# Adaptive max pooling over 1-D signals: the long store moves to ScalarE's queue, behind a 4-byte copy

## The chip, the cores and the metric

The kernel runs on one core of a Trainium2 chip. The metric is device time in microseconds (us), the median of several runs; three runs of the kernel before gave 334.86 to 335.0. The profile is one execution on the same kind of core, recorded by the hardware profiler.

## The reference

```python
batch, channels, length, output_size = 32, 256, 4096, 256
for i in range(output_size):
    start = int(i * length / output_size)
    end = int((i + 1) * length / output_size)
    result[:, :, i] = np.max(x[:, :, start:end], axis=-1)
```

The length is a multiple of the output size, so every output is the maximum of 16 neighbouring float32 values. The input has 134.2 MB, the output 8.4 MB.

## The kernel before

The input is looked at as 2,097,152 windows of 16 values. 128 partitions take 16,384 windows each; a "column" below is one window of every partition, so there are 16,384 columns to load, reduce and store.

The columns form two groups. Group A has 13,436 columns: a first small load of 128, twelve loads of 1024 and one of 1020. Group B has 2,948: two loads of 1024 and a last load of 900. In each group a partition's columns lie side by side in memory, so that a load, or a store, of a group is one DMA with 128 rows, one per partition, and each of the 16 DMA engines moves eight of the rows.

All loads are issued by SyncE (SP; line 87 for the first, line 96 for the others) into one SBUF tile, `ring`, which holds two full loads and two gaps of 152 columns. A load starts in one half of the ring, and every second time it is moved by the gap, so that it overlaps only a part of what the load two before it left there. VectorE (DVE) reduces each load with `pooled` (line 56) in two instructions, of 872 and 152 columns, in the order in which the load after next needs the space. A load is issued as soon as the larger of these two parts of the load two before it has been reduced. The maxima go to a second tile, `kept`; those of the last load (`last_kept`) go into free space of `ring`.

There are three stores. The long one holds group A's 13,436 columns (53,744 bytes per partition), the short one the two full loads of group B (2,048 columns), and the last one the last load's 900 columns. The first two are issued by SP at the end of the program, line 117, in the order in which `stores` lists them; the last one by ScalarE (ACT), line 114. On SP the long store stands directly behind the last load, since its own data is complete by then:

```python
    nc.scalar.dma_start(out=og[:, full : full + last], in_=last_kept)
    tc.no_sync_barrier()
    for dst, src in stores:
        nc.sync.dma_start(out=dst, in_=src)
```

`no_sync_barrier` keeps the order of the program's lines for the scheduler and adds no wait between engines. The profile calls SP's DMA queue q1 and ScalarE's q10.

Of the kernel before, what the change touches and what calls it, by code (L numbers as in the profile page):

```python
# [1 line left out]

# [4 lines left out]


@with_exitstack
def kernel(  # L10
    ctx: ExitStack,
    tc: tile.TileContext,
    x: bass.AP,
    output_size: bass.AP,
    out: bass.AP,
):

    nc = tc.nc
    P = nc.NUM_PARTITIONS
    fp32 = mybir.dt.float32

    B, C, L = x.shape
    O = int(output_size)  # L30
    assert L % O == 0, (L, O)
    W = L // O
    total = B * C * O // P
    assert B * C * O % P == 0

    CHUNK = 1024
    GAP = 152
    FIRST = 128
    LOADS_A, LOADS_B = 13, 2

    LESS = 4
    group_a = [FIRST] + [CHUNK] * (LOADS_A - 1) + [CHUNK - LESS]
    last = total - sum(group_a) - LOADS_B * CHUNK
    group_b = [CHUNK] * LOADS_B + [last]
    assert 0 < last and last * (W + 1) <= CHUNK * W

    pool = ctx.enter_context(tc.tile_pool(name="pool", bufs=1))
    ring = pool.tile([P, 2 * (CHUNK + GAP) * W], fp32, tag="ring", name="ring")
    kept = pool.tile([P, total - last], fp32, tag="kept", name="kept")

    xw = x.flatten_outer_dims().rearrange("r (o w) -> (r o) w", w=W)
    ow = out.flatten_outer_dims().rearrange("r o -> (r o)")

    def pooled(dst, at, n):

        nc.vector.reduce_max(  # L56
            out=dst,
            in_=ring[:, at * W : (at + n) * W].rearrange("p (n w) -> p n w", w=W),
            axis=mybir.AxisListType.X,
        )  # L60

    taken = 0

    def group(n):

        nonlocal taken
        span = slice(taken * P, (taken + n) * P)
        taken += n
        return (
            xw[span].rearrange("(p n) w -> p (n w)", p=P),  # L70
            ow[span].rearrange("(p n) -> p n", p=P),
        )

    stores = []
    n_loads = 0
    base = 0
    for g, loads in enumerate((group_a, group_b)):
        xg, og = group(sum(loads))
        a = sum(loads) if g == 0 else 0
        for n in loads:  # L80
            if g == 0:
                a -= n
            xn = xg[:, a * W : (a + n) * W]
            dst = kept[:, base + a : base + a + n] if n != last else None
            if n == FIRST:

                nc.sync.dma_start(  # L87
                    out=ring[:, CHUNK * W : (CHUNK + n) * W], in_=xn
                )
                pooled(dst, CHUNK, n)  # L90
            else:

                low = n_loads % 2 * (CHUNK + GAP)
                moved = n_loads // 2 % 2
                at = low + moved * GAP
                nc.sync.dma_start(out=ring[:, at * W : (at + n) * W], in_=xn)
                if n != last:
                    cut = CHUNK - GAP if moved else GAP
                    parts = [(0, cut), (cut, n)]
                    for u, v in parts if moved else parts[::-1]:  # L100
                        pooled(dst[:, u:v], at + u, v - u)
                else:
                    end = (at + CHUNK) * W
                    last_kept = ring[:, end - n : end]
                    pooled(last_kept, at, n)
                n_loads += 1
            if g:
                a += n
        full = a - last if g else sum(loads)
        stores.append((og[:, 0:full], kept[:, base : base + full]))  # L110
        base += full
    assert taken == total

    nc.scalar.dma_start(out=og[:, full : full + last], in_=last_kept)
    tc.no_sync_barrier()
    for dst, src in stores:
        nc.sync.dma_start(out=dst, in_=src)


# [1 line left out]
_INS = ['x', 'output_size']  # L121
_OUTS = [((32, 256, 256), 'float32')]

_NUMBERS = {'output_size': 256}


# [26 lines left out]
```

## Time and profile before

| | before |
|---|---|
| time, median of 3 runs | 334.9 us |
| span of the profiled execution, first to last instruction | 333.1 us |
| VectorE busy | 276.5 us (83%), 32 reductions |
| bytes over the DMA engines | 142.61 MB, mean 428 GB/s |
| the DMA engines' time in packets of q1 and q10 | 98.8% and 0.3% |
| one full load, from issue to landing | 24.0 us |
| the long store, from issue to landing | 37.2 us |
| the short store, from issue to landing | 18.1 us |
| the last store, from issue to landing | 4.2 us |

The span is all that the profile gives for its execution; the median of the runs lies 1.8 us above it. A time "from issue to landing" contains the time that a transfer stands in its queue behind others: the long store is issued 0.4 us after the last load and waits for it.

### The profile page before, as it was taken

What the parts mean: (1) busy time and instruction counts of PE and PEld (TensorE: products, weight loads), DVE (VectorE), ACT (ScalarE), POOL (GpSimd) and SP (SyncE); (2) the same over time, 40 slices, a digit from 0 to 9 for tenths busy, and PEclk for the clock granted to TensorE, in tenths of its full rate; (3) what the DMA queues carried; (4) which work ended last, traced back from release to release, by engine and by line L of the source; (5) the groups of instructions that cost most, each with busy time, mean ns of one, the idle gap of its engine ahead of it and who ended that gap; (6) DMA issues with size and microseconds to landing.
All of it is one profiled execution on the core that took longest, in us unless ns stands there. A gap on an engine that the chain in (4) does not pass through costs nothing.

```text
span 333.1 us, 113 instructions
## 1 busy us (share of the span) xinstructions
DVE 276.5 (83%) x32; POOL 0.2 (0%) x4
## 2 busy tenths in 40 slices
DVE  2009979797997979799797979979797998979993
POOL 0000000000000000000000000000000000000000
DMA  9898989899898989899898989899898989899996
GB/s 378 378 504 378 504 378 496 386 441 441 378 504 378 504 378 496 386 457 425 378 504 378 504 378 504 378 441 441 385 494 377 504 378 504 378 458 443 421 413 285
DMA packets 2880, 142.61 MB, mean 428 GB/s; under 512 B 320, under 2 KB 320, under 8 KB 448
## 3 DMA queue, kind: packets, MB, share of 16 engines
q1 hardware_dynamic: 2736, 142.15, 98.8%
q10 hardware_dynamic: 144, 0.46, 0.3%
HBM read 134.22 MB, written 8.39 MB: 428 GB/s over the span
## 4 chain that ended last, share of the span: by engine, by line
DMA 57%; DVE 36%; DVEq 5%; issue 0%; SPq 0%
DMA ring<-in_x_dram 57%; DVE kept L56 36%; DVEq L148 5%; SPq L87 0%
## 5 line engine op out<-in xcount | busy, mean ns | idle before, releaser
L56 DVE TENSOR_REDUCE kept<-ring 128x152 f32<-128x2432 f32 (+3 forms) x31 | 261.4, 8472 | 51.5 <-DMA ring<-in_x_dram 51.5
L56 DVE TENSOR_REDUCE ring<-ring 128x900 f32<-128x14400 f32 x1 | 15.1, 15144 | 0.0
L134 POOL MEMSET const-bfloat16-1.0<- 128x1 bf16 x1 | 0.1, 102 | 0.0
L134 POOL MEMSET const-uint8-127<- 128x1 uint8 x1 | 0.1, 102 | 0.0
L134 POOL MEMSET const-float32-0.0<- 128x1 f32 x1 | 0.1, 99 | 0.2 <-issue 0.2
L134 POOL MEMSET const-float32-1.0<- 128x1 f32 x1 | 0.1, 99 | 0.0
## 6 DMA issues: line engine op xcount, KB each, us to landing
ring<-in_x_dram SPq DMA_DIRECT2D x1, 8160.0 KB, 23.9
ring<-in_x_dram SPq DMA_DIRECT2D x1, 7200.0 KB, 21.6
out_dram<-kept SPq DMA_DIRECT2D x1, 6718.0 KB, 37.2
ring<-in_x_dram SPq DMA_DIRECT2D x1, 1024.0 KB, 4.7
out_dram<-kept SPq DMA_DIRECT2D x1, 1024.0 KB, 18.1
out_dram<-ring ACTq DMA_DIRECT2D x1, 450.0 KB, 4.2
ring<-in_x_dram SPq DMA_DIRECT2D x14, 24.0
```

Source lines behind the costliest of these rows:

```text
L56: nc.vector.reduce_max(out=dst, in_=ring[:, at * W : (at + n) * W].rearrange("p (n w) -> p n w", w=W), axis=mybir.AxisListType.X,)
L134: nc = _bacc.Bacc("TRN2", target_bir_lowering=False, num_devices=1)
L148: with _tile.TileContext(nc) as tc:
```

## The change

The long store moves from SP to ScalarE, and the last store from ScalarE to SP, behind the short one. The last full load (the one before the last load) is reduced in parts of 828 and 196 columns instead of 872 and 152. ScalarE first issues a DMA of 4 bytes, from the first column of that load's maxima to a new tile `gate`; it depends on the part of 828 columns, so ScalarE waits for that reduction. Behind it, ScalarE issues the long store. The long store has no dependency on the copy; only the order on ScalarE puts it behind.

```diff
+    gate = pool.tile([1, 1], fp32, tag="gate", name="gate")
...
+    OPEN = 828
...
                     cut = CHUNK - GAP if moved else GAP
+                    before_last = n_loads == LOADS_A + LOADS_B - 1
+                    if before_last:
+                        assert moved
+                        cut = OPEN
                     parts = [(0, cut), (cut, n)]
                     for u, v in parts if moved else parts[::-1]:
                         pooled(dst[:, u:v], at + u, v - u)
+                        if before_last and u == 0:
+                            nc.scalar.dma_start(out=gate[:, :], in_=dst[0:1, 0:1])
+                            tc.no_sync_barrier()
+                            nc.scalar.dma_start(out=stores[0][0], in_=stores[0][1])
...
-    nc.scalar.dma_start(out=og[:, full : full + last], in_=last_kept)
-    tc.no_sync_barrier()
-    for dst, src in stores:
-        nc.sync.dma_start(out=dst, in_=src)
+    nc.sync.dma_start(out=stores[1][0], in_=stores[1][1])
+    nc.sync.dma_start(out=og[:, full : full + last], in_=last_kept)
```

On VectorE the order of the instructions stays the same.

## The prediction

> **What bounds the kernel now.** I read the page first (shares of queues and engines), then windows over the whole span, then the timeline of the last 45 us, then the DMA queues in a short window near the end, and last the trace's DMA packet records (one for each row of a transfer on one DMA engine, with queue, start and duration) where a window is too coarse.
>
> The page, first the whole span and the engines, then the queues (packets, MB, share of 16 engines' span):
>
> ```profile
> span 333.1 us, 113 instructions
> DVE 276.5 (83%) x32; POOL 0.2 (0%) x4
> ...
> q1 hardware_dynamic: 2736, 142.15, 98.8%
> q10 hardware_dynamic: 144, 0.46, 0.3%
> ```
>
> q1 is SP's queue (all loads and two stores), q10 ScalarE's (the last store). Together they fill 99.1% of the 16 DMA engines' time over the whole span; VectorE has 17% to spare. The windows (us, DVE busy, POOL busy, clock, DMA share, GB/s) show where the other 1% is:
>
> ```profile
> 0.00:1.70 1.70, 0.00 (x0) 0.20 (x4) 1.00 0.00 0
> 1.70:2.70 1.00, 0.00 (x0) 0.00 (x0) 1.00 0.98 254
> 2.70:312.00 309.30, 260.50 (x31) 0.00 (x0) 1.00 1.00 434
> ...
> 331.70:333.06 1.36, 0.00 (x0) 0.00 (x0) 1.00 0.00 0
> ```
>
> It lies before the first packet and behind the last. In between, packet records show each engine's next row starting within 0.01 us of the end of the one before. So the span is a start of 1.7 us, a fixed amount of transfer at 434 GB/s until 331.71, 0.49 us until the last completion arrives (332.20) and 0.86 us of closing steps. Only three things can move the end: less transfer, an idle hole on the DMA engines, or a longer tail. The timeline shows what has to arrive in time for there to be no hole:
>
> ```profile
> 290.99 0.33 SPq L96 DMA_DIRECT2D ring<-in_x_dram  x1
> 291.37 21.91 SPq L117 DMA_DIRECT2D out_dram<-kept  x2
> 295.63 17.28 DVE L56 TENSOR_REDUCE kept<-ring 128x872 f32<-128x13952 f32 x2 [2.07 <-DMA ring<-in_x_dram]
> 312.82 15.14 DVE L56 TENSOR_REDUCE ring<-ring 128x900 f32<-128x14400 f32 x1
> 328.00 0.37 ACTq L114 DMA_DIRECT2D out_dram<-ring  x1
> ```
>
> The last load is issued at 290.99 and the long store 0.4 us behind it, on the same queue. By the packet records the load's eighth and last row on each engine starts at 309.50 to 310.02 and ends at 311.85 to 312.29; the load lands at 312.64. The long store then runs to 327.73 to 328.15, the short store (issued 312.94) to 330.21 to 330.60, and the last store to 331.71. It is issued at 328.00, after the last reduction, and its packets start on each engine where q1's end. This window of the queues lies wholly behind its issue:
>
> ```profile
> DMA packets 86, 0.70 MB, mean 414 GB/s; under 512 B 0, under 2 KB 0, under 8 KB 0
> ## 3 DMA queue, kind: packets, MB, share of 16 engines
> q1 hardware_dynamic: 86, 0.70, 98.8%
> ```
>
> No q10 packet runs in 328.5 to 330.2, though the first packet of the run came 1.00 us after its issue (0.73 to 1.73). The last store therefore stood ready behind q1's rows for about a second microsecond. That is the slack of the compute side: the last reduction could end some 0 to 1.2 us later without opening a hole.
>
> **The change part by part.** *Transfer.* The loads and the three stores keep their rows; each is one DMA, as before. Only the 4 B copy is new. Bytes saved: none, so nothing here gives a gain.
>
> *The 4 B copy.* It is one packet on one engine. The nearest rows are the 4 B completion writes, 0.009 us each (321 of them); the far bound is 0.91 us, the slowest packet of the run (an 8 KB row at the cold start). I take 0.01, by the size. No engine waits for the copy's data; the long store is issued behind it without waiting for its landing. The Trainium skill (DMA: Bandwidth & Descriptors, Specifications) says that a transfer under 512 B is done as a read-modify-write, which speaks against such a copy; no row here shows one, and it gives no figure.
>
> *The reductions.* The last full load is cut at 828 instead of 872 columns. From 14.686 us for 872 and 2.677 us for 152, a column costs 16.68 ns: 13.95 and 3.41 us, whose sum is unchanged at 17.36. The short store's wait and the last reduction's start (312.82) stay. Cost 0. The first part now ends at 295.63 + 13.95 = 309.58.
>
> *ScalarE's queue.* ScalarE waits for that end; behind the wait stands only the long store. A wait of this kind was followed by the issue 0.03 us later (327.97 to 328.00), an issue takes 0.37, and two issues follow each other 0.05 apart (1.10 to 1.15): copy at 309.61, long store at 310.03. Its first packets can run 1.00 us later, at 311.03 (start-up row); as an upper bound 2.21 later (328.00 to 330.21, a wait that the rows ahead explain), at 312.24. They are needed when the load's last row ends, from 311.85. The load's last row is therefore in progress on every engine when the store arrives, and the hole is 0 by the near bound and 0.39 us on the earliest engine by the far one (0.60 if that row, which ran up to 0.47 us over its usual 2.13, were not slowed). In the start-up the 16 engines' first rows were spread over 0.55 us, which puts the last arrival at 311.6, still early. I take 0.05. The cover is the load's last row; if it is gone, every microsecond of lateness is one of time. The Trainium skill (same page, Latency and other measured facts) gives a first byte of about 0.6 us for such a queue: behind the end of the issue (310.40) this is 311.0, no hole, and the sum would be 0.05 less. The start-up row agrees: 0.63 us from 1.10 to 1.73.
>
> *The slow last rows.* Ten of the 16 last load rows ran over, by 0.16 us in the mean over all 16. If the store's presence in the same queue causes it, up to 0.16 comes back; if not, 0. I take 0.
>
> *SP's queue.* It loses the long store's issue (0.43 us at 291.37, then a wait for VectorE until 312.9, so nothing came of it) and gets the last store behind the short one. The last store's issue still follows the last reduction at 328.0. Its queue mates: the short store's rows, on q1 from about 314, and the long store's on q10. In whatever order the engines serve them, they hold the same rows and run out at 330.21 to 330.60, when the last store has been ready for 0 to 1.2 us. Cost 0. What comes late next, if a hole opens, is exactly this last store.
>
> *The tail.* One more completion to be looked at: the closing waits that are already fulfilled cost 0.03 to 0.04 us each (332.26 to 332.29). I take 0.04.
>
> Sum: 0.01 + 0.05 + 0.04 = 0.10 on 333.06, so a span of 333.16. The median of the runs, 334.90, lies 1.84 above the span (there is no other time for the profiled execution), which gives 335.0. With the bounds of the hole and of the slow rows the forecast's own range is 334.7 to 335.6.
>
> **The rivals.** *A store row comes ahead of the load (slower).* With two queues an engine may take a 1.99 us row of the long store ahead of the load's last row, or ahead of the load's completion write. One engine is enough: the load lands at 314.63, the last reduction runs 314.81 to 329.95, the last store is issued at 329.98 and can run at 330.98 (or 332.19) at the earliest. The engines run out at 330.4 in the mean, so a hole of 0.6 to 1.8 us opens: 335.5 to 336.7. It decides from a landing over 0 to 1.2 us later than 312.64. For it: the store arrives some 0.6 us before the last rows end. Against it: at the end of before, rows and completion of the queue in hand all went ahead of q10. The Trainium skill (same page, Queues, rings and completion order) says that an engine changes queues only at a packet's end, typically 9 to 17 descriptors; eight rows and a completion would be one packet, which the tail agrees with. By that rule nothing gets between, and the time is the forecast's. Chance 0.14.
>
> *The copy or the hand-over is dear (slower).* The copy takes its far bound of 0.91 us on its engine, or the store comes over 0.7 us late. That engine finishes last: 335.8 to 336.0. Chance 0.07.
>
> *Two queues overlap on one engine (faster).* The store reads SBUF while the load writes it, so the store's first row could run beside the load's last: up to one row, 1.99 us, 332.9; half of it gives 333.9. For it: it would be the first time that a load and a store stand in two queues. Against it: where both queues were filled, rows of the one followed rows of the other without overlap, and the 434 GB/s is the same for loads (434) and the long store (433 in 311.84 to 327.73). The Trainium skill (same page, Issuing engines are not separate DMA queues) says that several queues interleave on the same 16 engines and gain no bandwidth; by that this chance would be 0. I give 0.07.
>
> *The holding back does not work.* If the store were issued when its own data is ready, before the last load, up to 15.9 us (its eight rows) would fall ahead of that load: about 350. Against it: in the program the copy carries the wait and stands before the store on ScalarE. Chance 0.02.
>
> **How the numbers follow.** The forecast has 0.70. I count 0.2% (0.67 us) as what a measurement of this kernel can tell from no change. Faster is the overlap, 0.07; slower is 0.14 + 0.07 + 0.02 = 0.23; the same is 0.70. The range is the forecast's, up through most of the first two rivals to 336.3, and down to 334.4, the slow rows' return with a little overlap; the deep overlap, the top of the first rival and the failed hold, under 2 in 10, are left out.
>
> **What would show it.** Right: DMA share still 1.00 to about 331.7, the long store's first rows starting within 0.01 us of the load's last, the last load landing at about 312.6, the last reduction ending at 328.0, the last store running last. The first rival: a landing at 314 or later, and a window near 330.5 with a low DMA share. The dear hand-over: a hole at 311.9 to 312.5. Overlap: over 434 GB/s around 312 and an end before 331. Wrong altogether: if the end moves over 0.7 us with the DMA engines as full as before and the same landing.

## The result and the profile after

The changed kernel takes 335.63 us, median of 17 runs, against 334.96 for 17 runs of the kernel before beside them: 1.0017 times as long, with a 95% interval of 1.0011 to 1.0024 (the medians themselves stand at 1.0020). It is slower, by 0.67 us between the medians and 0.4 to 0.8 us by the interval. The forecast was 335.0 in a range of 334.4 to 336.3. The profiled span grew by 0.84 us, from 333.06 to 333.90.

The page of the changed kernel, whole span and queues. The long store's bytes have moved from q1 to q10; VectorE works as long as before:

```profile
span 333.9 us, 114 instructions
DVE 276.5 (83%) x32; POOL 0.2 (0%) x4
...
q1 hardware_dynamic: 2736, 135.73, 94.2%
q10 hardware_dynamic: 146, 6.88, 4.8%
```

The timeline around the end of the last load (start, duration, engine, line, operation):

```profile
295.87 17.28 DVE L57 TENSOR_REDUCE kept<-ring 128x828 f32<-128x13248 f32 x2 [2.07 <-DMA ring<-in_x_dram]
309.86 1.13 ACTq L113 DMA_DIRECT2D gate<-kept  x1
311.03 1.08 ACTq L115 DMA_DIRECT2D out_dram<-kept  x1
313.06 15.14 DVE L57 TENSOR_REDUCE ring<-ring 128x900 f32<-128x14400 f32 x1
...
328.23 0.34 SPq L129 DMA_DIRECT2D out_dram<-ring  x1
```

The copy is issued when forecast (309.86 for 309.61, in an execution in which the last load was issued 0.24 us later too), but its issue lasts 1.13 us and the long store's 1.08, where 0.37 had been taken for the first. The windows (us, DVE busy, POOL busy, clock, DMA share, GB/s) show what this does. A packet counts in full where it starts, so that a short window can show a share far above 1:

```profile
2.70:311.80 309.10, 260.06 (x31) 0.00 (x0) 1.00 1.00 433
311.90:312.60 0.70, 0.70 (x1) 0.00 (x0) 1.00 0.01 0
312.60:332.42 19.82, 15.61 (x2) 0.00 (x0) 1.00 0.99 423
332.42:333.90 1.48, 0.00 (x0) 0.00 (x0) 1.00 0.00 0
```

Between 311.90 and 312.60 no row starts. By the packet records the load's last rows end at 311.89 to 312.42 (mean 312.07), and the first long rows start at 312.62 to 312.76 (mean 312.67): all 16 engines stand still, 0.60 us in the mean. The kernel before has 998 GB/s booked in the same 0.70 us:

```profile
311.90:312.60 0.70, 0.70 (x1) 0.00 (x0) 1.00 2.32 998
```

After that the engines are full to the end. They alternate between the queues row by row: from 318.6 on each engine does one long row (1.99 us), then one row of the short store (0.31 us). The queues (packets, MB, share of 16 engines) in the stretch from 316 to 330 of the changed kernel, both at work:

```profile
q10 hardware_dynamic: 96, 5.16, 85.4%
q1 hardware_dynamic: 80, 0.66, 11.0%
```

The 0.84 us of the spans can be followed through the mean ends of the rows. The load's last rows end 0.02 us later, the hole adds 0.60, and the long rows take 15.99 instead of 15.89 us in all. The short store's rows take 0.02 less and the last store's 0.03 more, which makes 0.73; the last packets end 0.75 later in the mean. The latest of them ends only 0.70 later (332.41 instead of 331.71), since the engines end closer together than before. The last landing is 0.69 later (332.89 instead of 332.20), and from there to the end it is 1.01 us instead of 0.86: 0.69 + 0.15 = 0.84.

### The profile page after: what moved, and what is told of

It is laid out like the page before. It is cut to its first block, busy times and chain, and to the rows that moved or that the text cites. A ratio compares the mean times of both kernels' runs of the same rounds, so it can differ in the third digit from the quotient of the medians.

```text
span 333.9 us, 114 instructions
## 1 busy us (share of the span) xinstructions
DVE 276.5 (83%) x32; POOL 0.2 (0%) x4
## 4 chain that ended last, share of the span: by engine, by line
DMA 57%; DVE 36%; DVEq 5%; issue 0%; SPq 0%
DMA ring<-in_x_dram 57%; DVE kept L57 36%; DVEq L160 5%; SPq L93 0%
## 5 line engine op out<-in xcount | busy, mean ns | idle before, releaser
L57 DVE TENSOR_REDUCE kept<-ring 128x152 f32<-128x2432 f32 (+5 forms) x31 | 261.4, 8473 | 51.7 <-DMA ring<-in_x_dram 51.7
```

The source lines that it names most:

```text
L57: nc.vector.reduce_max(out=dst, in_=ring[:, at * W : (at + n) * W].rearrange("p (n w) -> p n w", w=W), axis=mybir.AxisListType.X,)
```

## The experiments

All times are medians beside runs of the kernel before on the same chip. The open question was what opens the hole: that the store comes late, that ScalarE issues it, the copy, or the second queue. ScalarE and its queue q10 go together in every run here, so those two can't be told apart.

**An earlier store.**

```diff
-    OPEN = 828
+    OPEN = 764
```

> The last full load is cut at 764 columns instead of 828, so that the 4 B copy and the long store are issued 64 x 16.68 ns = 1.07 us earlier. Late hand-over (my theory: in the changed kernel the DMA engines stood still from 311.9 to 312.6 because the long store's first rows came too late): first long rows ready by 311.6, no hole, the span 0.6 us shorter and the time 335.0 to 335.1, within 0.2 of the kernel before. Rival, a store row ahead of the load: the earlier store gets rows in front of the load's last ones, the last load lands about 2 us later and the time is 335.6 or more. Rival, two queues cost something by themselves: the hole goes but the time stays at 335.6.

Measured: 335.95 against 335.09, ratio 1.0026 (1.0016 to 1.0035). The hole is gone and the time has not come back. The issues are earlier as planned, and the long rows start at 311.75 to 312.43, directly behind the load's; but these first 16 rows last 2.84 us in the mean instead of 1.99. The timeline, then windows; no row starts in 312.60 to 314.40, since all the first ones are still under way:

```profile
308.88 1.13 ACTq L113 DMA_DIRECT2D gate<-kept  x1
310.05 0.48 ACTq L115 DMA_DIRECT2D out_dram<-kept  x1
```

```profile
311.90:312.60 0.70, 0.70 (x1) 0.00 (x0) 1.00 3.52 1075
312.60:314.40 1.80, 1.80 (x2) 0.00 (x0) 1.00 0.00 0
```

They end at 314.54 to 315.19; in the changed kernel, with the store issued 1 us later, they ended at 314.64 to 314.79. So the expectation's third branch held, the hole gone and the time still high. Lateness, as I had put it, isn't the whole cause: 0.86 us of slow first rows took the place of 0.60 us of hole. The load landed on time (312.94), so no row had got ahead of it.

**The copy on ScalarE itself.**

```diff
-                            nc.scalar.dma_start(out=gate[:, :], in_=dst[0:1, 0:1])
+                            nc.scalar.copy(out=gate[:, :], in_=dst[0:1, 0:1])
```

> The hold is made by a one-element copy that ScalarE computes itself, in place of the 4 B DMA; the cut stays at 828. Late hand-over: the DMA copy's issue, 1.13 us on ScalarE, is gone, and the store's issue begins about 310.1 instead of 311.0. If the store's own issue stays at 1.08 us, its first rows run at about 311.7 and the hole is 0 to 0.1; if the 1.08 was caused by the copy in front and falls to 0.4, they are ready at 311.0. Either way 335.0 to 335.2. Rival, two queues cost something by themselves: 335.6 as with the DMA copy.

Measured: 336.03 against 335.09, 1.0028 (1.0017 to 1.0038). The timeline, then windows:

```profile
309.94 0.37 ACTq L115 DMA_DIRECT2D out_dram<-kept  x1
```

```profile
311.90:312.60 0.70, 0.70 (x1) 0.00 (x0) 0.00 (x0) 1.00 3.66 1152
312.60:314.40 1.80, 1.80 (x2) 0.00 (x0) 0.00 (x0) 1.00 0.00 0
```

The store's issue begins at 309.94 and lasts 0.37 us. The long issue is gone with the copy, though the run before had 0.48 us with the copy in front. Yet the first long rows last 2.74 us, and the time is no better than with the copy. The price needs no 4 B DMA.

**A copy on all 16 engines.**

```diff
-    gate = pool.tile([1, 1], fp32, tag="gate", name="gate")
+    gate = pool.tile([P, 1], fp32, tag="gate", name="gate")
...
-                            nc.scalar.dma_start(out=gate[:, :], in_=dst[0:1, 0:1])
+                            nc.scalar.dma_start(out=gate[:, :], in_=dst[:, 0:1])
```

> The copy takes one column of all 128 partitions (512 B on 16 engines) instead of 4 B on one engine. If the copy's issue is long (1.13 us) because it runs on one engine only, it falls to about 0.4 us, the long store comes 0.7 us earlier, the hole closes and the time is 335.0 to 335.2. If any DMA that ScalarE issues at this moment takes 1.1 us, the issues and the hole stay and the time is 335.6 or slightly more (8 packets more on each engine, 0.009 us each).

Measured: 336.15 against 335.09, 1.0031 (1.0019 to 1.0043).

```profile
310.08 0.49 ACTq L113 DMA_DIRECT2D gate<-kept  x1
310.62 2.27 ACTq L115 DMA_DIRECT2D out_dram<-kept  x1
```

The copy's issue falls to 0.49 us, as it should if one engine alone makes it long; but the store's issue behind it rises to 2.27 us, the first long rows start at 313.39 and the hole grows to 1.28 us. Neither branch of the expectation held whole: a shorter issue of the copy doesn't bring the store earlier.

**A much earlier store.**

```diff
-    OPEN = 828
+    OPEN = 400
```

> The last full load is cut at 400 columns: copy and long store are issued 428 x 16.68 ns = 7.14 us earlier, when about three rows of the last load are still to come on each engine. If the engines alternate between the queues row by row, with one or two rows of the load already in hand, one or two long rows (1.99 us each) get ahead of the load's last rows: the load lands 2 to 4 us later (314.9 to 316.9), the last reduction ends that much later, and the hole moves to the end: 335.7 to 338.4. If an engine first finishes all eight rows of a transfer (my reading of the kernel before), the load lands at 312.9 as now and the time is 335.0 to 335.1.

Measured: 339.37 against 335.09, 1.0127 (1.0113 to 1.0141). The engines alternate row by row. The first long rows, 1.99 us each, start from 307.73 between rows of the load, two get ahead on most engines, and the load's completion waits for another one: its rows end by 316.47, its last completion arrives at 318.83. That is about a row more than the expectation had counted (a landing up to 316.9), and the time is beyond its 338.4. The timeline, and a window without DMA work near the end, while VectorE still reduces:

```profile
303.87 0.47 ACTq L115 DMA_DIRECT2D out_dram<-kept  x1
...
318.93 15.15 DVE L57 TENSOR_REDUCE ring<-ring 128x900 f32<-128x14400 f32 x1 [5.82 <-DMA ring<-in_x_dram]
334.11 0.34 SPq L129 DMA_DIRECT2D out_dram<-ring  x1
```

```profile
330.90:334.90 4.00, 3.18 (x1) 0.00 (x0) 1.00 0.00 0
```

This shows what the hold is for. It also shows long rows of 1.985 us right behind rows of the load on another queue: here, with the store issued 3.9 us before its first row, going from one queue to the other costs nothing.

**A store one row ahead.**

```diff
-    OPEN = 828
+    OPEN = 608
```

> The cut at 608 columns issues copy and long store 220 x 16.68 ns = 3.67 us earlier than the changed kernel, so that the store can be taken about 308.2 (issue at about 307.4 plus what the earlier cuts showed), while the seventh or eighth row of the last load runs. Theory from the runs at 764 and 400 (an engine chooses its next row one row ahead, and alternates between the queues): no hole and no slow first row, but on some or all engines the load's last row or its completion write comes behind the first long row; the load lands at 314.5 to 315.0 instead of 312.9, the last reduction ends at about 330.0, the hole moves to the end, and the time is 335.5 to 336.4. If there is a cut that costs nothing, this should be near it: landing 312.9 and 335.0.

Measured: 335.50 against 335.04, 1.0012 (1.0003 to 1.0021). As expected: no hole, first long rows of 1.99 us, all load rows ahead of them; but 15 of the 16 completions of the load arrive at 314.31 to 314.89, behind the first long row. The last reduction starts at 314.99, ends at 330.14, and the engines run dry before the last store:

```profile
314.99 15.15 DVE L57 TENSOR_REDUCE ring<-ring 128x900 f32<-128x14400 f32 x1 [1.84 <-DMA ring<-in_x_dram]
330.17 0.34 SPq L129 DMA_DIRECT2D out_dram<-ring  x1
```

```profile
330.40:331.00 0.60, 0.00 (x0) 0.00 (x0) 1.00 0.05 14
```

**The same hold on SP's queue**, first with the cut at 764, then with the changed kernel's 828. `held` is where the maxima of the last full load go.

```diff
                 nc.sync.dma_start(out=ring[:, at * W : (at + n) * W], in_=xn)
+                if n == last:
+                    tc.no_sync_barrier()
+                    nc.sync.dma_start(out=gate[:, :], in_=held[0:1, 0:1])
+                    tc.no_sync_barrier()
+                    nc.sync.dma_start(out=stores[0][0], in_=stores[0][1])
...
                         if before_last and u == 0:
-                            nc.scalar.dma_start(out=gate[:, :], in_=dst[0:1, 0:1])
-                            tc.no_sync_barrier()
-                            nc.scalar.dma_start(out=stores[0][0], in_=stores[0][1])
+                            held = dst
```

> Copy and long store are issued by SP, on the loads' own queue, behind the last load; the cut is 764, so the store is issued at about 310.0 to 310.5 as in the run with that cut on ScalarE; all stores go over SP. If the cost (first long rows of 2.84 us instead of 1.99) comes from a late arrival of the rows, it is here too: about 335.8. If it comes from the change of queue at the end of the load, the first rows take 1.99 us and the time is 335.0 to 335.2.

Measured: 335.28 against 335.04, 1.0006 (0.9997 to 1.0015).

> The changed kernel with only the queue undone: cut at 828, 4 B copy and long store as there, but both issued by SP behind the last load. By SP's issue times at the cut of 764 (0.70 and 0.35 us) the store is issued at about 310.6, 0.4 us before the changed kernel's. Theory, that the price is the change of queue at the end of the load and not the hold: no hole, first rows of about 1.99 us, 335.1 to 335.4, not to be told from the kernel before. Rival, that a hold until this late opens the hole on any queue: first long rows at 312.3 or later, 335.6 or more.

Measured: 335.21 against 335.06, 1.0006 (0.9997 to 1.0015). In both, first long rows of 1.99 us start with no hole behind the load's. With the cut at 828, the timeline and windows:

```profile
309.88 0.71 SPq L105 DMA_DIRECT2D gate<-kept  x1
310.65 0.35 SPq L107 DMA_DIRECT2D out_dram<-kept  x1
```

```profile
311.90:312.60 0.70, 0.70 (x1) 0.00 (x0) 1.00 2.68 1152
312.60:314.40 1.80, 1.80 (x2) 0.00 (x0) 1.00 1.04 448
```

This comparison decides. At 310.65 the store is issued 0.6 us later than in the run with the cut at 764 on ScalarE (310.05), and 0.7 us later than with ScalarE's own copy at the same cut (309.94), and there is neither a hole nor a slow row. A hold until then costs nothing that these runs can tell from the kernel before; held back on ScalarE and its queue it does. It doesn't try SP's queue as late as the changed kernel's store, whose issue ended at 312.11 instead of 311.00 here: the hole of that kernel goes with the late end of ScalarE's issue, and the slow rows are the price of the runs that were in time.

**A queue that has run before.** The cut is 764, everything else as in the changed kernel.

```diff
+    warm = pool.tile([P, W], fp32, tag="warm", name="warm")
+    nc.scalar.dma_start(
+        out=warm[:, :], in_=xw[0 : P].rearrange("(p n) w -> p (n w)", p=P)
+    )
```

> As the run with the cut at 764, with one more load of 8 KB (128 rows of 64 bytes, unused) on ScalarE's queue at the start, so that this queue has run on all 16 engines before the long store. If the first long rows are slow because their queue is used for the first time, they fall from 2.84 to 1.99 us and the time to 335.1 or 335.2 (the added load costs under 0.1 us). If not, 335.9 to 336.0 as with that cut.

Measured: 335.95 against 335.04, 1.0027 (1.0017 to 1.0037), first long rows of 2.86 us. First use of the queue is not the cause.

**The last store alone moved.**

```diff
-    nc.scalar.dma_start(out=og[:, full : full + last], in_=last_kept)
-    tc.no_sync_barrier()
     for dst, src in stores:
         nc.sync.dma_start(out=dst, in_=src)
+    nc.sync.dma_start(out=og[:, full : full + last], in_=last_kept)
```

> The kernel before, with the last store alone moved from ScalarE to SP, behind the short one; no copy, no hold, the long store on SP as before. By the late hand-over nothing but the closing differs: 335.0 to 335.2, with up to 0.15 us for the order of the closing waits. If the last store's place on SP had cost a part of the 0.6 us of the whole change, it would be 335.3 or more.

Measured: 335.22 against 335.04, 1.0003 (0.9994 to 1.0012). This part of the change is not to be told from nothing.

**Short rows in front**, with the cut at 608.

```diff
-                            nc.scalar.dma_start(out=stores[0][0], in_=stores[0][1])
+                            for v0, v1 in ((0, 512), (512, sum(group_a))):
+                                nc.scalar.dma_start(
+                                    out=stores[0][0][:, v0:v1], in_=stores[0][1][:, v0:v1]
+                                )
```

> As the run with the cut at 608, but ScalarE stores group A in two DMAs, first 512 columns (rows of 2 KB), then the other 12,924. Theory: an engine that has the other queue's row on hand one row ahead takes it between the load's last row and the load's completion write; what that costs is the length of that one row. With rows of 2 KB (about 0.08 us, from 0.31 us for 8 KB) instead of 1.99 us, the load lands at 312.6 to 313.1, the last reduction starts by 313.3, no row is slow and no hole opens: 335.1 to 335.3, against 335.5 with long rows in front. If the completions wait for something else (the whole long store's share, or a fixed time after a change of queue), the load lands at 314 or later, and the time is 335.5 or more.

Measured: 335.39 against 335.13, 1.0009 (1.0000 to 1.0018). The load's completions now come behind one row of 0.08 us; the last one lands at 313.05, and the last reduction starts at 313.14 instead of 314.99:

```profile
307.92 4.60 ACTq L116 DMA_DIRECT2D out_dram<-kept  x1
313.14 15.15 DVE L57 TENSOR_REDUCE ring<-ring 128x900 f32<-128x14400 f32 x1
```

So what the completions waited for is one row of the other queue, and a short one costs them little. The time, 335.39, is just above the 335.1 to 335.3 expected. It isn't free: ScalarE's second issue lasted 4.60 us, to 312.52, and its first rows started at 313.08 in the mean, some 0.2 us after the eight short ones.

**Both kernels again.**

> The changed kernel once more, unchanged, on the same chip as the split store, to see how far the hole repeats: the DMA engines idle from 311.9-312.4 to about 312.6, first long rows of 2.03 us, and 0.5 to 0.8 us over the kernel before.

Measured: 335.97 against 335.13, 1.0026 (1.0016 to 1.0035). The hole repeats and is larger, 0.87 us, with a store issue of 1.39 us. The same kernel thus cost 0.67 and 0.84 us in two comparisons, so a difference of 0.2 us or less between two of the versions above says nothing.

```profile
310.96 1.39 ACTq L115 DMA_DIRECT2D out_dram<-kept  x1
```

> The kernel before once more, for a second profile: which parts of the 0.84 us between the two spans are repeated. The start-up and the last rows of the last load may differ by 0.1 to 0.3 us; the long store's first rows start within 0.01 us of the load's last ones, and from the last landing to the end it is 0.86 us.

Measured: 335.13 in a single run, span 333.35, which is 0.29 us above the first profile's; no hole. The load's last rows ran over by 0.02 us in the mean here and by 0.16 in the first profile, so most of that is scatter. From the last landing to the end it is 0.86 us again.

## Why the prediction was right, and where it was not

**What bounds the kernel** was right: transfer and VectorE's work are unchanged, and the change shows as idle time of the DMA engines. That nothing in it can give a gain held in every run: no version here was faster than the kernel before.

**The number** lies in the range, but not by the sum: 0.10 us had been added up, 0.67 us came. 335.63 is at the upper end of the forecast's own range (335.6), which only the far bound of the hand-over reaches; the lower end comes to 334.8 by its terms, not 334.7. The rise is just as large as the 0.2% (0.67 us) that the prediction counts as no change, and that it fell on this side is luck. Of the signs named for the forecast, the full DMA engines outside the hole, the landing (312.86) and the last store running last came true; the long rows directly behind the load's didn't, and the hole at 311.9 to 312.5, named as the sign of a dear hand-over, did come.

**The hand-over** was the mis-sized term: 0.05 taken, 0.60 measured in the first profile and 0.87 in the second. Its durations were taken from the wrong rows. The issue of a one-row DMA lasted 1.13 us, not 0.37 (0.71 on SP, 0.49 for 128 rows), and the store's behind it 1.08. From the store's issue to its first row it was 1.59 us, between the bounds of 1.00 and 2.21, where I took 1.00. The Trainium skill's first byte of 0.6 us (DMA: Bandwidth & Descriptors, Latency and other measured facts) is near the 0.51 us from the end of that issue to the first row; what came late was the end of the issue.

More important, the step "needed when the load's last row ends" was wrong for a second queue. With the store issued 1 us earlier, in time by that step, its first rows lasted 0.75 to 0.88 us longer (three runs: the cut at 764, ScalarE's own copy, the queue that has run before); on the loads' own queue, issued at 309.56 and 310.65, they didn't (two runs). On the second queue the first rows were neither late nor slow only where the store was issued more than a row earlier, and then the completion fell behind a long row (cuts 608 and 400). That an engine chooses one row ahead, and has to begin anew for a row that comes after this choice, fits these runs but isn't shown: the records show when rows start and end, not when they are fetched.

**The 4 B copy** cost its engine 0.009 us, as taken (of the 321 records of 4 B that the prediction calls completion writes, 320 are). Its long issue delayed the store in the changed kernel; yet without it the time was no better (336.03), and on SP the same copy cost nothing that can be told. The **reductions** cost nothing, as forecast. The **slow last rows** gave no lasting gain: they were gone in the changed kernel, but nearly gone in the second profile of the kernel before too. The **tail** was 0.15 instead of 0.04 us: in the kernel before, the last store's completion was asked for in the third of SP's four closing waits, in the changed one in the first, so that three more followed it instead of one. They begin 0.07 us apart (332.90, 332.97, 333.04, 333.11); the 0.03 that the prediction read was only the length of one. The kernel with only the queue undone shows the same 0.15: its last landing is at 332.50, as in the second profile of before (332.49), its end at 333.51 instead of 333.35. With the last store alone moved it is 0.99 us from the last landing to the end (332.62 to 333.61), so the tail goes with that store's place.

**The rival of a store row ahead** did not occur at this cut, but its mechanism and its price are real: with the cut at 608 a landing at 314.9, the engines idle for 0.6 us in the mean before the last store, and 335.50, at the lower end of its 335.5 to 336.7. My evidence against it was a misreading. I took it that the last store stood ready while q1 finished its whole share. Engines alternate row by row, so the lack of q10 rows in 328.5 to 330.2 more likely says that it was not ready: the 1.6 us found here from a ScalarE issue to its first row would be 329.6, only two rows of 0.31 us before q1's end. By this estimate the slack was 0.6 to 1.0 us, inside the 0 to 1.2 that I had given, but not for the reason given. The Trainium skill's rule (same page, Queues, rings and completion order) of a change of queue after a packet of typically 9 to 17 descriptors, as I had applied it, doesn't fit these traces: the engines changed queues after every row (1.99 and 0.31 us in turn), and between a load's last row and its completion write.

**The dear hand-over**, with a chance of 0.07, is in kind what came: the hole was 0.60 us in the first profile and 0.87 in the second, on either side of the 0.7 that I had set for it. Overlap of load and store was not seen in any run, and the hold itself worked.

## What to carry to other kernels

When the DMA engines are full, look for the point where one stream hands over to the next: rows queued behind it on the same queue followed without a gap here, even when issued only 1.2 us ahead of need; on a second queue they were, at every cut tried here, late, or slow, or ahead of the first stream's completion. So to hold back a transfer, try first to queue it behind the one that it must follow rather than time it from an engine's progress. Before an issue is costed, look for a row of the same form, on the same engine and with the engines as busy; one of another form was wrong here by a factor of three.

## What the hardware showed that I had not expected

A DMA's issue can last far longer than the 0.33 to 0.43 us of most: 1.13 us for one row on ScalarE, 1.08, 1.39, 2.27 and 4.60 us for a DMA behind another one on ScalarE while the engines were busy with the load, but also 0.48 in between (cuts 764, 608, 400). The four longest end 0.14 to 0.20 us after the last packet of the copy ahead of them on the same queue had run (in the changed kernel 312.11 after 311.93), but at the cut of 764 the issue ended 1.6 us before that packet. What decides stays open. The completion write of a load can stand behind a row of another queue: it came one row later, 1.99 us or 0.08.
